# Second attention of a two-layer decoder trunk: filler remainders flushed together in mid head, one filler step ahead of transposes, Newton steps of two scalings moved

## Chip, cores and metric

One Trainium2 chip, one core. The metric is the time of one execution of the whole program in device microseconds, lower is better.

## What is computed

The reference is a decoder trunk of two layers over one sequence of 512 tokens with width 1024, in float32. Each layer has a token mixer and then a gated MLP with a causal convolution of width 3; each sub-layer starts with an RMS norm that is shifted and scaled by a vector c, and ends in a gated addition to x. The mixer of layer 0 is a stick-breaking attention. The mixer of layer 1, which the change is mostly about, is a sparse attention with an indexer:

```python
def dsa_attention(h, w_in, q_gain, k_gain, w_uv, w_out, rel_bias):
    proj = h @ w_in
    q, lat, qi, ki, wi = jnp.split(proj, [o1, o2, o3, o4], axis=-1)
    q = rms_norm(q.reshape(B, S, DSA_HEADS, DSA_LATENT), q_gain)
    k = rms_norm(lat, k_gain)
    ...
    logits = jnp.einsum('bqhd,bqkd->bqhk', qb, kg) * scale
    logits = logits + bias
    logits = jnp.where(valid[:, :, None, :], logits, NEG)
    p = jax.nn.softmax(logits, axis=-1)
    o_lat = jnp.einsum('bqhk,bqkd->bqhd', p, vg)
    ...
    o = jnp.einsum('bshl,hlv->bshv', o_lat, w_uv)
    return o.reshape(B, S, DSA_HEADS * DSA_V_DIM) @ w_out
```

There are 16 heads with a latent of 128. The query of each head is normalized over its 128 channels (`q_gain` goes into the keys), and the indexer picks 128 keys for each token.

## The kernel before

x stands transposed in SBUF, 8 tiles of 128 channels by 512 tokens. Every product with a weight is done as three matmuls (`mm3`, L247 to L250): weight and activation are each split into a high part and the remainder, and high by high, low by high and high by low are added up in PSUM. Weights come as chunks of 128x1024 by DMA; `split_hi` (L199) makes a chunk's high part on ScalarE, `split_lo` (L212) its low part, on VectorE or, where it is told so, on GpSimd. The order of the instructions of each engine is the order in which the code issues them; nothing reorders them later.

The program is a chain of `stick_layer`, `ffn_layer`, `dsa_layer`, `ffn_layer`. Between two of them stands `boundary` (L387, three times): the last product of a sub-layer in two halves of 256 tokens with 8 tiles each (`out_tile`, which adds to x by `add_to_x` on VectorE and squares on ScalarE), and beside it the next norm. The first half's norm is a seed on ScalarE (`norm_seed`, L324), one Newton step of three VectorE operations on 128x256 (`norm_newton`, L330) and 10 operations of a generator (`norm_ops`), of which a tuple says how many stand behind each tile of the second half. The mean squares of the second half are gathered in quarters by matmuls (`quarter_squares`, L300), which go on with the last four tiles' squares beside the next layer's first product.

The attention loop of `dsa_layer` (L1476) runs over 16 heads and is pipelined by a head. In the pass of head h, TensorE makes the logits of head n = h+1 in four row blocks j of 128 tokens by 128(j+1) keys (`logits`, three matmuls each; they use the two banks `z` in turn), and transposes head h's exponentials in three groups (`transposed`; the copy out of PSUM goes to ScalarE, VectorE, ScalarE). VectorE scales the logits by the query's factor, adds bias and mask and takes the row's maximum (`softmax`, L1372: L1376 and L1377); ScalarE makes the exponential and its row sum (`expo`, L1379). The factor is a column of `cols`, made by `q_norm` (L1129) from sums of squares: a seed on ScalarE and four VectorE operations on 128x16. GpSimd adds the mask to the biases of head h+2 behind each transposed group (`masked_bias`, L1350).

Two heads make a pair. In even heads from 2 on, `weighted` multiplies the previous pair's transposed exponentials by its values; `pair_values` stands in odd heads. The reciprocals of the row sums of a pair are spread out by a VectorE copy (`pair_sums`, L1429, tile `rvb`), transposed in `pair_scale` and multiplied in by `pair_hi`; `pair_lo` (VectorE, L1453, in odd heads from 3 on) makes the low part.

Where the loop calls `fill(n)`, n steps of the generator `late_steps` (L1317) are issued. A step is one `mm3`. The generator first makes the query projections of heads 12 to 15 (8 steps each, the first two of head 12 stand ahead of the loop), then the first half of the output projection (8 tiles of 4 steps). What has to follow each of these is put into the list `events`: behind a query `q_hi` (ScalarE: copy and square), `q_lo` (VectorE) with the next chunk's `split_hi`, and `split_lo` on GpSimd; behind the four queries `group_sum(3)`, `group_columns(3)` and `q_norm(12, 16)`; behind an output tile `add_to_x`. `fill` takes one event off the list after each step:

```python
def fill(n):
    for _ in range(n):
        next(filler, None)
        if events:
            events.pop(0)()
```

`LATE_STEPS` (L39) gives the number of steps of each head; half of them stand in mid head, ahead of the logits of block 2, the rest at its end.

Of the kernel before, what the change touches and what calls it, by code (L numbers as in the profile page):

```python
# [22 lines left out]
QT = S // P  # L23
# [4 lines left out]
HEADS = 16  # L28
# [9 lines left out]
EARLY_Q = 12  # L38
LATE_STEPS = [3, 3, 3, 3, 3, 2, 3, 3, 3, 4, 4, 4, 4, 4, 4, 4]  # L39
AHEAD = 2  # L40
# [77 lines left out]
def kernel_body(ctx, tc, xT, wst, cst, smalls, crow, ccol, relb, onehot, outT):  # L118
# [205 lines left out]
    def norm_seed(hf):  # L324
        ln = rstd[hf] = npool.tile([P, H2], F32, name="ln", bufs=2)
        act.activation(ln, sqs["pt"], AF.Abs_reciprocal_sqrt, bias=eps_c)
        rstd[hf, "ms"] = sqs["pt"]
# [59 lines left out]
    def boundary(last, O, l, gate, nxt, first):  # L387
# [51 lines left out]
        for m in range(KT):  # L439
            if m == 1:  # L440
                sum_squares(sqs["acc"], True, False)
                sum_squares(prev, False, True)
                norm_seed(0)
            if m == 5:
                quarter_squares(pend[:4], True)
            pend.append(out_tile(1, m))
            if m == 1:
                norm_newton(0)
            if m in (2, 4):
                split_hi()  # L450
            if m in (3, 5):
                split_lo()
            for _ in range((0, 0, 1, 1, 2, 1, 2, 2)[m]):
                next(ops0, None)
# [5 lines left out]
        hs, c = hcur["h"], halves[0]  # L460
# [599 lines left out]
    def dsa_layer(l, first, man):  # L1060
        with ExitStack() as st:
# [66 lines left out]

            def q_norm(h0, h1):  # L1129
                c = slice(h0 * QT, h1 * QT)  # L1130
                act.activation(rq[:, c], msq[:, c], AF.Abs_reciprocal_sqrt, bias=eps_c)
                dve.tensor_mul(r0q[:, c], rq[:, c], rq[:, c])
                dve.scalar_tensor_tensor(r0q[:, c], msq[:, c], EPS, r0q[:, c], op0=OP.add, op1=OP.mult)
                dve.scalar_tensor_tensor(rq[:, c], r0q[:, c], 3.0, rq[:, c], op0=OP.subtract, op1=OP.mult)
                dve.tensor_scalar(rq[:, c], rq[:, c], -0.5 * P ** -0.5, None, op0=OP.mult)

            ths = {}
# [6 lines left out]
            with ExitStack() as si:  # L1144
# [115 lines left out]
                steps = 2 * rounds  # L1260
# [47 lines left out]
            with ExitStack() as sa:  # L1308
# [8 lines left out]
                def late_steps():  # L1317

                    g, pt = late, late_pt
                    for h in range(EARLY_Q, HEADS):  # L1320
# [3 lines left out]
                        for _ in g:  # L1324
                            yield
                        events.extend([lambda h=h, pt=pt: q_hi(h, pt), lambda h=h, pt=pt: (q_lo(h, pt), split_hi()),
                                       lambda: split_lo(engine=pool)])
                    events.extend([lambda: group_sum(3), lambda: group_columns(3), lambda: q_norm(EARLY_Q, HEADS)])
                    for mp in range(4):
# [12 lines left out]
                def fill(n):  # L1342
                    for _ in range(n):
                        next(filler, None)
                        if events:
                            events.pop(0)()

# [112 lines left out]
                for j in range(QT):  # L1460
                    logits(0, j)
                    fill(1)
                    softmax(0, j)
                    if j == 0:
                        group_columns(2)
                        q_norm(8, EARLY_Q)
                        warm(AF.Exp)
                    expo(0, j)
                rvb = None

# [5 lines left out]
                for h in range(HEADS):  # L1476
# [9 lines left out]
                    if values:  # L1486
                        weighted(h - 2)
                    transposed(h, 0, True)
                    if more:
# [4 lines left out]
                    if not more:  # L1494
                        rvb = sums(h)
                        pair_values(h - 1)
                    fill(LATE_STEPS[h] // 2)
                    if more:
# [17 lines left out]
                    else:  # L1516
                        pair_scale(rvb)
                    fill(LATE_STEPS[h] - LATE_STEPS[h] // 2)
                    if values:
# [3 lines left out]
                pair_lo()  # L1523
                fill(100)
                first = boundary([("do", 1, m) for m in range(4)], O[4:], l, 2, (l, S_NF, 3, 4), up_first(l))
# [117 lines left out]
```

## Time and profile before

| | |
|---|---|
| Runs | 1291.43, 1288.93, 1291.10 us; median 1291.1 |
| The profiled execution | 1289.12 us |
| Its span | 1287.3 us, granted TensorE clock 1.00 |
| TensorE busy | 1267.7 us, 98% of the span, 6910 matmuls |
| VectorE busy | 930.0 us, 72% |
| ScalarE busy | 592.0 us, 46% |
| GpSimd busy | 103.4 us, 8% |
| DMA | 163.22 MB, 127 GB/s in the mean |

Times count from the start of the span. "Busy" is the time in which an engine executes an instruction; the weight loads of TensorE run beside its matmuls. The attention loop lies between about 760 and 895 us, the three boundaries near 260, 630 and 910 us.

### The profile page before, as it was taken

Reading aid. Unit: us, or ns where it says so; the run is one execution under the profiler, and the core shown is the slowest. Engines: PE = TensorE matmul, PEld = TensorE weight load, DVE = VectorE, ACT = ScalarE, POOL = GpSimd, SP = SyncE. Lnnn points to the kernel's source line nnn. Section 1 sums busy time; section 2 is a strip of 40 time slices with the busy share of each in tenths; the row PEclk is TensorE's granted clock in tenths of the full one; section 3 lists DMA queues with packets and bytes.
Section 4 is the critical chain, followed back from the end, with each engine's and each line's share of the span. In section 5 each row is a group of like instructions: output and inputs, shape, how many; then the busy total and the mean of one; then the engine's idle time right before and its main releaser. Section 6 shows DMA issues by size and latency. Waiting matters only on the chain.

```text
span 1287.3 us, 18011 instructions
## 1 busy us (share of the span) xinstructions
PE 1267.7 (98%) x6910; PEld 1054.8 (82%) x6910; DVE 930.0 (72%) x1528; ACT 592.0 (46%) x1051; POOL 103.4 (8%) x99
## 2 busy tenths in 40 slices
PE   8999999999999999999999999999999999999999
PEld 6988787898888888888897777767988888888888
DVE  5888988778777877885778897776876456456653
ACT  6576666454423323442555346654554334234430
POOL 0000000000000000000002355453000000000000
PEclk9999999999999999999999999999999999999999
DMA  9644434423575575654222212231322422423221
GB/s 374 212 131 132 140 124 126 136 66 117 194 250 188 181 239 191 195 177 151 83 66 82 82 50 58 66 120 52 92 86 74 127 86 74 128 89 98 75 90 66
DMA packets 50613, 163.22 MB, mean 127 GB/s; under 512 B 5808, under 2 KB 8624, under 8 KB 50528
## 3 DMA queue, kind: packets, MB, share of 16 engines
q1 hardware_dynamic: 50096, 161.30, 39.0%
q8 instruction: 54, 0.88, 0.3%
q10 hardware_dynamic: 432, 0.79, 0.2%
q14 instruction: 31, 0.25, 0.1%
HBM read 159.92 MB, written 2.14 MB: 126 GB/s over the span
## 4 chain that ended last, share of the span: by engine, by line
PE 89%; DVE 6%; ACT 2%; DMA 2%; issue 1%; SPq 0%; DVEq 0%; ACTq 0%
PE pt_u L248 11%; PE pt_u L249 11%; PE pt_u L250 11%; PE pt_d L248 5%; PE pt_d L249 5%; PE pt_d L250 5%; PE pt_first L248 2%; PE pt_first L249 2%; PE pt_first L250 2%; PE pt_q L248 2%; PE pt_qk L248 2%; PE pt_q L250 2%; PE pt_q L249 2%; PE pt_l L249 2%; PE pt_l L248 2%; PE pt_l L250 2%
## 5 line engine op out<-in xcount | busy, mean ns | idle before, releaser
L208 ACT ACTIVATE whi<-raw 128x1024 fp32r<-128x1024 f32 (+1 forms) x206 | 205.3, 1002 | 116.7 <-PE pt_d L250 93.2
L248 PE MATMUL pt_u<-hhi,whi 128*128 128x512 f32 x640 | 249.2, 389 | 0.0
L249 PE MATMUL pt_u<-hhi,wlo 128*128 128x512 f32 x640 | 249.0, 389 | 0.0
L250 PE MATMUL pt_u<-hlo,whi 128*128 128x512 f32 x640 | 249.0, 389 | 0.0
L216 DVE TENSOR_TENSOR wlo<-raw,whi 128x1024 fp32r<-128x1024 f32 (+1 forms) x186 | 213.9, 1151 | 14.1 <-ACT whi L208 13.3
L996 ACT ACTIVATE y<-pt_u,sm 128x512 f32<-128x512 f32 x80 | 62.2, 777 | 188.3 <-PE pt_u L250 188.3
L248 PEld LDWEIGHTS pt_u<-hhi,whi 128*128 128x128 f32 x640 | 120.1, 188 | 25.9 <-issue 1.1
L250 PEld LDWEIGHTS pt_u<-hlo,whi 128*128 128x128 f32 x640 | 120.1, 188 | 25.2
L249 PEld LDWEIGHTS pt_u<-hhi,wlo 128*128 128x128 f32 x640 | 120.1, 188 | 24.6
L997 DVE SCALAR_TENSOR_TENSOR y<-pt_u,sm,y 128x511 f32<-128x511 f32 x80 | 59.9, 748 | 97.1 <-ACT y L996 96.9
L248 PE MATMUL pt_d<-acthi,whi 128*128 128x512 f32 x288 | 112.0, 389 | 0.0
L249 PE MATMUL pt_d<-acthi,wlo 128*128 128x512 f32 x288 | 112.0, 389 | 0.0
L250 PE MATMUL pt_d<-actlo,whi 128*128 128x512 f32 x288 | 112.0, 389 | 0.0
L257 DVE SCALAR_TENSOR_TENSOR raw<-raw,cond 128x1024 f32<-128x1024 f32 x88 | 106.6, 1217 | 4.4 <-DMA raw<-wst 4.4
L370 DVE SCALAR_TENSOR_TENSOR x<-pt_d,mod,x 128x512 f32<-128x512 f32 x48 | 36.0, 750 | 72.8 <-PE pt_d L250 72.8
L232 ACT ACTIVATE acthi<-y 128x512 fp32r<-128x512 f32 x44 | 27.8, 632 | 105.4 <-DVE y L1015 105.4
L248 PE MATMUL pt_first<-hhi,whi 128*128 128x256 f32 (+1 forms) x224 | 68.2, 305 | 0.0
L249 PE MATMUL pt_first<-hhi,wlo 128*128 128x256 f32 (+1 forms) x224 | 67.1, 300 | 0.7 <-DVE wlo L216 0.7
L250 PE MATMUL pt_first<-hlo,whi 128*128 128x256 f32 (+1 forms) x224 | 66.9, 299 | 0.0
L250 PEld LDWEIGHTS pt_d<-actlo,whi 128*128 128x128 f32 x288 | 54.1, 188 | 11.3
L248 PEld LDWEIGHTS pt_d<-acthi,whi 128*128 128x128 f32 x288 | 54.1, 188 | 11.2
L249 PEld LDWEIGHTS pt_d<-acthi,wlo 128*128 128x128 f32 x288 | 54.1, 188 | 11.1
(252 smaller groups left out, 2691.7 us busy)
## 6 DMA issues: line engine op xcount, KB each, us to landing
raw<-wst SPq DMA_DIRECT2D x250, 512.0 KB, 3.7
raw<-wst SPq DMA_DIRECT2D x48, 384.0 KB, 3.0
th<-rb SPq DMA_DIRECT2D x16, 256.0 KB, 3.4
ada<-wst SPq DMA_DIRECT2D x4, 512.0 KB, 6.3
outT<-x SPq DMA_DIRECT2D x16, 128.0 KB, 1.7
x<-xT SPq DMA_DIRECT2D x5, 256.0 KB, 5.0
x<-xT ACTq DMA_DIRECT2D x3, 256.0 KB, 3.9
cond<-crow SPq DMA_DIRECT2D x1, 512.0 KB, 10.7
```

What stands on the lines that cost most here:

```text
L208: act.activation(hi[:, :n], raw[:, :n], AF.Copy)
L216: engine.tensor_sub(lo[:, :n], raw[:, :n], hi[:, :n].bitcast(F32))
L232: act.activation(hi, src, AF.Copy)
L248: pe.matmul(out, lhsT=whi, rhs=ahi, start=start, stop=False)
L249: pe.matmul(out, lhsT=wlo, rhs=ahi, start=False, stop=False)
L250: pe.matmul(out, lhsT=whi, rhs=alo, start=False, stop=stop)
L257: dve.scalar_tensor_tensor(raw, raw, 1.0, cond, op0=OP.mult, op1=OP.mult, accum_out=dst)
L370: dve.scalar_tensor_tensor(x[f][:, c], pt, mod[l][:, g * KT + f:g * KT + f + 1], x[f][:, c], op0=OP.mult, op1=OP.add)
L996: act.activation(y, pt, AF.Identity, scale=cw[2], bias=sm[:, b + S_CB + c:b + S_CB + c + 1])
L997: dve.scalar_tensor_tensor(y[:, 1:], pt[:, :S - 1], cw[1], y[:, 1:], op0=OP.mult, op1=OP.add)
```

## The change

- `fill` no longer takes events. A new function `flush` runs the events up to the next separator (`None`) in the list. It is called once in each head, in mid head ahead of the first fill, and a second time at the end of heads 9 and 10. Separators stand around `group_sum(3)`, `group_columns(3)` and `q_norm(12, 16)`, so that each flush does one of them.
- In heads without `weighted` (0 and the odd ones) one filler step stands ahead of the first group of transposes; it is taken from the head's number of steps. `LATE_STEPS` changes in heads 0, 4 and 6; its sum stays 54.
- `q_norm` is cut into `q_seed` and `q_newton`; for heads 8 to 11 the four VectorE operations move from the first block of head 0's logits behind the last one.
- In `boundary` the Newton step of the first half moves from behind the second half's tile 1 to directly behind the seed, ahead of the residual add of tile 1, and the tuple of operations behind the tiles changes.

```diff
--- before.py
+++ after.py
@@ -36,7 +36,7 @@
 H2 = S // 2
 QRING = 12
 EARLY_Q = 12
-LATE_STEPS = [3, 3, 3, 3, 3, 2, 3, 3, 3, 4, 4, 4, 4, 4, 4, 4]
+LATE_STEPS = [4, 3, 3, 3, 2, 3, 2, 3, 3, 4, 4, 4, 4, 4, 4, 4]
 AHEAD = 2
 FETCH = 1
 
@@ -441,16 +441,15 @@
                 sum_squares(sqs["acc"], True, False)
                 sum_squares(prev, False, True)
                 norm_seed(0)
+                norm_newton(0)
             if m == 5:
                 quarter_squares(pend[:4], True)
             pend.append(out_tile(1, m))
-            if m == 1:
-                norm_newton(0)
             if m in (2, 4):
                 split_hi()
             if m in (3, 5):
                 split_lo()
-            for _ in range((0, 0, 1, 1, 2, 1, 2, 2)[m]):
+            for _ in range((0, 1, 1, 1, 2, 1, 2, 1)[m]):
                 next(ops0, None)
         for _ in ops0:
             pass
@@ -1126,13 +1125,20 @@
                 act.activation(msq[:, 16 * g:16 * g + 16].rearrange("p (i j) -> p i j", i=4),
                                pt.rearrange("p (j i r) -> p i j r", j=QT, i=4)[:, :, :, 0], AF.Copy)
 
-            def q_norm(h0, h1):
+            def q_seed(h0, h1):
                 c = slice(h0 * QT, h1 * QT)
                 act.activation(rq[:, c], msq[:, c], AF.Abs_reciprocal_sqrt, bias=eps_c)
+
+            def q_newton(h0, h1):
+                c = slice(h0 * QT, h1 * QT)
                 dve.tensor_mul(r0q[:, c], rq[:, c], rq[:, c])
                 dve.scalar_tensor_tensor(r0q[:, c], msq[:, c], EPS, r0q[:, c], op0=OP.add, op1=OP.mult)
                 dve.scalar_tensor_tensor(rq[:, c], r0q[:, c], 3.0, rq[:, c], op0=OP.subtract, op1=OP.mult)
                 dve.tensor_scalar(rq[:, c], rq[:, c], -0.5 * P ** -0.5, None, op0=OP.mult)
+
+            def q_norm(h0, h1):
+                q_seed(h0, h1)
+                q_newton(h0, h1)
 
             ths = {}
 
@@ -1325,7 +1331,8 @@
                             yield
                         events.extend([lambda h=h, pt=pt: q_hi(h, pt), lambda h=h, pt=pt: (q_lo(h, pt), split_hi()),
                                        lambda: split_lo(engine=pool)])
-                    events.extend([lambda: group_sum(3), lambda: group_columns(3), lambda: q_norm(EARLY_Q, HEADS)])
+                    events.extend([None, lambda: group_sum(3), None, lambda: group_columns(3), None,
+                                   lambda: q_norm(EARLY_Q, HEADS)])
                     for mp in range(4):
                         whi, wlo = chunk(("do", 0, mp), 0)
                         for mi in range(2):
@@ -1342,8 +1349,14 @@
                 def fill(n):
                     for _ in range(n):
                         next(filler, None)
-                        if events:
-                            events.pop(0)()
+
+                def flush():
+
+                    while events:
+                        event = events.pop(0)
+                        if event is None:
+                            return
+                        event()
 
                 Ls = {}
 
@@ -1463,9 +1476,10 @@
                     softmax(0, j)
                     if j == 0:
                         group_columns(2)
-                        q_norm(8, EARLY_Q)
+                        q_seed(8, EARLY_Q)
                         warm(AF.Exp)
                     expo(0, j)
+                q_newton(8, EARLY_Q)
                 rvb = None
 
                 def sums(h):
@@ -1485,6 +1499,8 @@
                         expo(n, 0)
                     if values:
                         weighted(h - 2)
+                    else:
+                        fill(1)
                     transposed(h, 0, True)
                     if more:
                         softmax(n, 1)
@@ -1494,7 +1510,9 @@
                     if not more:
                         rvb = sums(h)
                         pair_values(h - 1)
-                    fill(LATE_STEPS[h] // 2)
+                    flush()
+                    steps = LATE_STEPS[h] - (not values)
+                    fill(steps // 2)
                     if more:
                         logits(n, 2)
                         softmax(n, 2)
@@ -1515,13 +1533,21 @@
                             load_bias(n + 3)
                     else:
                         pair_scale(rvb)
-                    fill(LATE_STEPS[h] - LATE_STEPS[h] // 2)
+                    if h in (9, 10):
+                        flush()
+                    fill(steps - steps // 2)
                     if values:
                         pair_hi()
                 weighted(HEADS - 2)
                 pair_hi()
                 pair_lo()
-                fill(100)
+                while events:
+                    flush()
+                for _ in filler:
+                    while events:
+                        flush()
+                while events:
+                    flush()
                 first = boundary([("do", 1, m) for m in range(4)], O[4:], l, 2, (l, S_NF, 3, 4), up_first(l))
         return first, man
 
```

In the following pieces `L` is a row block of logits and exponentials, `z` a bank of logits, `tr` a bank of transposes, `pt_q` the accumulator of a query projection, `q2l` its square, `whi` and `wlo` a weight chunk's two parts. The line numbers of the change are those of its own file.

TensorE in head 1, from the logits of head 2's block 1 on. Before:

```order
L1367 MATMUL z<-kph,qh 128x256
L1368 MATMUL z<-kph,ql 128x256
L1369 MATMUL z<-kpl,qh 128x256
L1391 MATMUL tr<-cons,L_7183 128x128
L1391 MATMUL tr<-cons,L_7185 128x128
L1391 MATMUL tr<-cons,L_7187 128x128
L1391 MATMUL tr<-cons,L_7189 128x128
L248 MATMUL pt_q<-hhi,whi 128x512
L249 MATMUL pt_q<-hhi,wlo 128x512
L250 MATMUL pt_q<-hlo,whi 128x512
```

With the change:

```order
L1380 MATMUL z<-kph,qh 128x256
L1381 MATMUL z<-kph,ql 128x256
L1382 MATMUL z<-kpl,qh 128x256
L248 MATMUL pt_q<-hhi,whi 128x512
L249 MATMUL pt_q<-hhi,wlo 128x512
L250 MATMUL pt_q<-hlo,whi 128x512
L1404 MATMUL tr<-cons,L_7183 128x128
L1404 MATMUL tr<-cons,L_7185 128x128
L1404 MATMUL tr<-cons,L_7187 128x128
L1404 MATMUL tr<-cons,L_7189 128x128
```

A step of the query projection that stood behind the first group of transposes (and others behind it) now stands between the logits and these transposes.

ScalarE from the end of head 0 to the exponential of head 2's block 2, in head 1. Before:

```order
L1381 ACTIVATE L_7189,sum<-L_7189,nm 128x512
L1088 ACTIVATE qh<-pt_q 128x512
L1089 ACTIVATE q2l<-pt_q 128x512
L1381 ACTIVATE L_7268,sum<-L_7268,nm 128x128
L1396 ACTIVATE pT<-tr 128x512
L1381 ACTIVATE L_7289,sum<-L_7289,nm 128x256
L208 ACTIVATE whi<-raw 128x1024
L1381 ACTIVATE L_7300,sum<-L_7300,nm 128x384
```

With the change:

```order
L1394 ACTIVATE L_7189,sum<-L_7189,nm 128x512
L1394 ACTIVATE L_7271,sum<-L_7271,nm 128x128
L1409 ACTIVATE pT<-tr 128x512
L1394 ACTIVATE L_7292,sum<-L_7292,nm 128x256
L1087 ACTIVATE qh<-pt_q 128x512
L1088 ACTIVATE q2l<-pt_q 128x512
L208 ACTIVATE whi<-raw 128x1024
L1394 ACTIVATE L_7303,sum<-L_7303,nm 128x384
```

The copy and the square of head 12's query, which stood ahead of head 2's first exponential, stand behind its second one, directly ahead of the split of the next weights.

GpSimd in head 1: the mask additions for head 3, and the low part of that weight chunk. Before:

```order
L1354 TENSOR_TENSOR L_7342<-th,maskb 128x128
L1354 TENSOR_TENSOR L_7366<-th,maskb 128x256
L1354 TENSOR_TENSOR L_7388<-th,maskb 128x384
L1354 TENSOR_TENSOR L_7390<-th,maskb 128x512
L216 TENSOR_TENSOR wlo<-raw,whi 128x1024
L1354 TENSOR_TENSOR L_7434<-th,maskb 128x128
```

With the change:

```order
L1367 TENSOR_TENSOR L_7343<-th,maskb 128x128
L216 TENSOR_TENSOR wlo<-raw,whi 128x1024
L1367 TENSOR_TENSOR L_7374<-th,maskb 128x256
L1367 TENSOR_TENSOR L_7396<-th,maskb 128x384
L1367 TENSOR_TENSOR L_7398<-th,maskb 128x512
L1367 TENSOR_TENSOR L_7437<-th,maskb 128x128
```

The low part of the weights stands behind the first mask addition, where it stood behind the fourth.

## Rows read from the trace of the kernel before

Each row of a timeline has the start in us, the duration in us, engine, line, operation, out<-in, the number of equal instructions in a row, and in brackets the idle time before it with what ended it.

**Rows 1.** The chain that ended last: shares of the span by engine.

```profile
PE 89%; DVE 6%; ACT 2%; DMA 2%; issue 1%; SPq 0%; DVEq 0%; ACTq 0%
```

**Rows 2.** Windows, attention: length; busy PE, PEld, DVE, ACT, POOL; clock; DMA share; GB/s.

```profile
760.00:895.00 135.00, 125.81 (x770) 98.33 (x769) 98.89 (x202) 81.93 (x216) 67.28 (x70) 1.00 0.23 71
```

**Rows 3.** Waits of TensorE, whole span: waiter <- releaser: idle sum, number, longest.

```profile
PE z L1367 <- DVE L L1376: 6.4, 8, 1.5
PE pt_part L305 <- ACT sqt L285: 3.0, 3, 1.0
PE tr L1391 <- ACT L L1381: 2.5, 4, 0.8
```

**Rows 4.** Timeline of TensorE: logits of block 3 that wait.

```profile
763.24 0.50 PE L1367 MATMUL z<-kph,qh 128*128 128x512 f32 x1 [1.28 <-DVE L L1376]
...
815.68 0.40 PE L250 MATMUL pt_q<-hlo,whi 128*128 128x512 f32 x1
817.60 0.44 PE L1367 MATMUL z<-kph,qh 128*128 128x384 f32 x1 [1.52 <-DVE L L1376]
```

**Rows 5.** Timeline of VectorE: a Newton operation of the query scales, first and last set.

```profile
760.69 1.09 DVE L1133 SCALAR_TENSOR_TENSOR cols<-cols 128x16 f32<-128x16 f32 x1
...
848.03 0.18 DVE L1133 SCALAR_TENSOR_TENSOR cols<-cols 128x16 f32<-128x16 f32 x1
```

**Rows 6.** Timeline of TensorE, heads 2 and 3.

```profile
783.47 0.48 PE L1367 MATMUL z<-kph,qh 128*128 128x512 f32 x1
...
785.16 0.40 PE L248 MATMUL pt_q<-hhi,whi 128*128 128x512 f32 x1
...
785.85 0.22 PE L1367 MATMUL z<-kph,qh 128*128 128x128 f32 x1
...
786.54 0.88 PE L1391 MATMUL tr<-cons,L 128*128 128x128 f32 x4
...
788.83 0.48 PE L1367 MATMUL z<-kph,qh 128*128 128x512 f32 x1
...
790.50 0.38 PE L1391 MATMUL tr<-cons,L 128*128 128x128 f32 x2
```

**Rows 7.** Timeline of ScalarE: last exponentials of a head; a query's square; a split.

```profile
786.22 0.72 ACT L1381 ACTIVATE L<-L,nm 128x512 f32<-128x512 f32 x1 [0.57 <-DVE nm L1377]
...
831.79 0.72 ACT L1381 ACTIVATE L<-L,nm 128x512 f32<-128x512 f32 x1 [0.57 <-DVE nm L1377]
...
834.88 0.59 ACT L1089 ACTIVATE q2l<-pt_q 128x512 f32<-128x512 f32 x1
835.36 1.06 ACT L208 ACTIVATE whi<-raw 128x1024 fp32r<-128x1024 f32 x1
```

**Rows 8.** Timeline of VectorE: heads 3 and 9.

```profile
790.67 0.43 DVE L1431 COPY rvb<-rv 128x512 f32<-128x512 f32 x1
...
835.50 0.69 DVE L1095 TENSOR_TENSOR ql<-pt_q,qh 128x512 fp32r<-128x512 f32 x1 [1.12 <-ACT q2l L1089]
...
838.02 1.43 DVE L1431 COPY rvb<-rv 128x512 f32<-128x512 f32 x1
...
839.37 0.74 DVE L1376 SCALAR_TENSOR_TENSOR L<-z,cols,L 128x512 f32<-128x512 f32 x1
```

**Rows 9.** Timeline of GpSimd and VectorE: a split of weights and what fell into it.

```profile
817.04 2.39 POOL L216 TENSOR_TENSOR wlo<-raw,whi 128x1024 fp32r<-128x1024 f32 x1 [1.73 <-issue]
...
818.63 1.35 DVE L1453 TENSOR_TENSOR olo<-bs,ohi 128x512 fp32r<-128x512 f32 x1
```

**Rows 10.** Timeline of ScalarE: table load ahead of the last query scales' seed.

```profile
846.11 1.28 ACT L1131 ACT_TABLE_LOAD   x1
```

**Rows 11.** Timeline of ScalarE and VectorE, third boundary: norm seed, residual adds.

```profile
908.93 0.46 ACT L326 ACTIVATE ln<-pt_norm,ecols 128x256 f32<-128x256 f32 x1
...
910.33 0.48 DVE L370 SCALAR_TENSOR_TENSOR x<-pt_l,mod,x 128x256 f32<-128x256 f32 x1 [1.82 <-PE pt_l L250]
...
921.76 0.48 DVE L370 SCALAR_TENSOR_TENSOR x<-pt_l,mod,x 128x256 f32<-128x256 f32 x1
```

## The prediction

> **What bounds the kernel now.** I read the chain that ended last first: TensorE holds 89% of it and no other engine more than 6% [rows 1]. So a microsecond counts only where TensorE stands still. Next, the windows: of the 135 us of the second attention TensorE is busy 125.8, at a granted clock of 1.00 [rows 2]. Then who waited for whom on TensorE [rows 3]: logits wait 8 times for VectorE's read of the block that last held their bank (6.4 us), transposes wait 4 times for ScalarE's exponential (2.5 us), and the quarter sums of the boundaries wait 3 times for a square (3.0 us). All twelve attention waits lie in the stretch that the change rearranges. A wait costs a little more than its idle time: from 815.68 to 817.60 is 1.92, where the usual pitch is 0.23, so 1.69 are lost for 1.52 shown [rows 4]. Twelve waits are thus 8.9 + 12 x 0.16 = 10.8 us. Five more odd heads end their first transposes about 0.2 late (786.54 to the next logits, 788.83, is one [rows 6]), 1.1 in all. **11.9 us** is what the change can win in the attention, less what waits remain or are new.
>
> **What it wins.** Query scales: at 760.69 a step of the Newton chain takes 1.09 where the same shape later takes 0.18 [rows 5], the logits of block 3 wait 1.28 behind it [rows 4]. With the four steps behind the last block's softmax that wait goes, and so do the two smaller ones that follow from it; the chain then stands beside a filler step. Step ahead of transposes: one step of three products is 0.69 (785.16 to 785.85 [rows 6]), no wait of the transposes is over 0.8 [rows 3]; so these four and the five small ones go, nearly. I leave 0.4 for all of them. The number of filler steps is the same, so TensorE's own work is.
>
> **What takes their place: odd heads.** After heads 1, 3, 7 and 9 a query projection is finished, and its copy, square, low part and the split of the next weights now stand together in mid head, ahead of the softmax of block 2. I follow head 9 of before, which already has that order. ScalarE: from the exponential of the last block (831.79) to the end of the square (834.88 + 0.59) is 3.7 [rows 7]. I take 3.9, since the copy of the transposes that precedes it comes behind one more filler step. VectorE can't start the low part earlier (835.50, right at the square's end), and block 2's and 3's softmax stand behind it: 2.52 from there to the copy `rvb` (838.02), 0.35 for that undisturbed (790.67 takes 0.43), 0.75 for the read of block 3 [rows 8]. So block 3's bank is free 3.9 + 2.5 + 0.35 + 0.8 = 7.6 after that exponential.
>
> On top comes GpSimd. Its split of weights takes 2.39, and a VectorE operation with both inputs in SBUF that fell into it (818.63) took 1.35, ending just after it [rows 9]; `rvb` at 838.02 took 1.43 for 0.43 in the same way, behind one of GpSimd's mask additions [rows 8]. The new order puts that split ahead of the masks, right behind ScalarE's split, which ends 0.95 after the square (835.36 + 1.06 [rows 7]). It then runs from 0.95 to 3.35 after the square, and `rvb` wants to start 2.55 after it: 0.8 more. Freed after **8.4**.
>
> TensorE's way to the product that needs this bank, from the logits of block 3 in the even head before [rows 6]: they, two transposes and a step 1.69; a second step 0.69; two logits 0.69; the inserted step 0.70; first transposes to the next block 3 2.29 less the 0.2 wait; that block and the values 1.67; transposes and one step (1.69 less 0.77) 0.92; a logit 0.28: 8.7. The exponential starts 2.75 after the same logits (783.47, 786.22 [rows 6, 7]), so TensorE arrives 6.0 after it. Before, such an odd head ended with two steps; the inserted one was taken from there. Wait: 8.4 - 6.0 = **2.4 in heads 1 and 3**. Head 7 follows a head with one step less: **3.1**. Head 9 keeps two steps and the sums ahead, as now, so I take a wait not far above the longest logits wait of now, 1.52 [rows 4]: **1.8**.
>
> **Heads 10 and 11.** The last query scales move from mid head to its end. There ScalarE needs a table load of 1.28 [rows 10] right behind the last exponential: 0.8 (as 831.79 [rows 7]) + 1.28 + 0.3 for a small seed, then on VectorE the Newton chain 0.8 (four steps as 848.03 [rows 5]), a residual add and the pair's scaling 1.3 (two operations of the low part's shape, 0.69 each) and block 0's read 0.35 (half of block 3's 0.74 [rows 8]), that is 4.85 after an exponential that started 2.75 behind its logits: 7.6. TensorE arrives with block 2 at about 4.9 (1.69 + 0.69 + 0.69 + 0.70 + transposes 0.4 + a step 0.75): **2.7**. The other table load delays that head's splits, and block 3's bank comes 1.0 late, or 2.0 if `rvb` falls into GpSimd's split (the two start within 0.3 of each other): **1.5**. Rows show no block longer than 1.0, and I go by that. The Trainium skill's page SBUF — State Buffer, section Who interferes with whom, says that the pair of ports is held for the whole instruction and the other engine fully blocks. By that rule head 11 could lose 3.0 in place of 1.5, and the total would be 1.5 higher.
>
> Head 13 gets a split and two residual adds in mid head: **0.6**. At the end of the loop nothing moves that TensorE waits for.
>
> **Boundaries.** VectorE idles 1.82 before 910.33 while the seed is there from 908.93 + 0.46 on [rows 11]; the three Newton steps, 1.25, move into it. But the first seven counts of the table now sum to 8, not 7, so one more pair of operations (0.8) stands ahead of the last residual add (921.76), whose square the quarter sums wait for, and 0.5 of the freed time goes into waiting for residuals that TensorE hasn't finished. Net about +0.1 each, +0.3 for three. Bounds: -0.5 (no waiting) to +0.8 (the move yields nothing) each.
>
> **Sum.** Left and new in the attention: 0.4 + 2.4 + 2.4 + 3.1 + 1.8 + 2.7 + 1.5 + 0.6 = 14.9. Against 11.9, and with +0.3: **+3.3 us**. The profiled execution took 1289.1, so 1292.4; the median of the runs, 1291.1, is 2.0 above it, so **1294.4**. Ends of the unknown: without any block by GpSimd the odd heads give 1.6 + 1.6 + 2.3 + 1.0, heads 11 and 13 1.0 and 0.1, together 10.7 and a net of -0.9; with head 11 at 2.0 and the boundaries at their worst +5.9.
>
> **Rivals.** First, *odd heads keep up* (faster). If the query's square ended 1.5 after the exponential, not 3.9, nothing would wait in heads 1, 3 and 7. Head 1 of before carries the same copies without a wait, which speaks for it; against it, they stand there ahead of the next head's first exponential and of the transposes' copy, now behind both. The 7.9 us would go: 1294.4 - 7.9 = 1286.5. It takes over from the point at which the low part starts before block 2's logits are done. Chance 0.20. Second, *an even trade*: the blocks don't happen, as with the `rvb` copy of 790.67 [rows 8], and the net is -0.9: 1290.2. Chance 0.30. Third, *the clock*: TensorE drops to the lower of its levels after a wait of 2.5 to 3 us. Now it is 1.00 across all waits up to 1.5 [rows 2, 3]. If it halved for the 8 us of one even head, that head would take 8 more: 1302. Chance 0.04. The Trainium skill's page TensorE: Matmul & The Clock Gate, section HAM oscillation, describes such drops after idle gaps; no run here shows one. The forecast, waits moved into odd heads, has 0.46; its own range is 1292 to 1297.5.
>
> **How the numbers follow.** About 0.2% of 1291.1, 2.6 us, is what a measurement of this kernel can tell from no change. Slower by more, above 1293.7: 0.36 of the forecast's 0.46 and the clock's 0.04, 0.40. Within: 0.10 of the forecast and 0.27 of the even trade, 0.37. Faster, below 1288.5: the first rival and 0.03 of the second, 0.23. The range leaves out half of the first rival and the far ends above: 1287 to 1297.5.
>
> **What would show it.** Right: TensorE's waits of logits on VectorE grow from 6.4 us, the longest at the second logits of heads 2, 4, 8 and at block 2 of head 11, while transposes wait almost nowhere and the start of the attention is some 2.7 us shorter; `rvb` copies of over 1 us beside GpSimd's splits in odd heads; quarter sums still near 3.0. Wrong: logits waits below 4 us, or a low part of the query that starts ahead of block 2's logits; then the first rival holds. If waits at heads 2, 4 and 8 are 1.5 each and no `rvb` is long, the second.

## The result

The changed kernel takes 1298.53 us (median of four runs, 1296.89 to 1299.11), the kernel before 1290.46 beside it (1288.93 to 1291.43): ratio 1.0062, 95% interval 1.0044 to 1.0079. It is slower, as forecast, but by 8.1 us where +3.3 was forecast, and outside the range that ended at 1297.5. The two profiled executions are 9.9 apart (1299.02 and 1289.12 us). Up to the first logits of the attention 1.0 of this has arisen (they start at 758.93, before at 757.93): 0.8 by 41 us of the program, in waits for parts of the first weight chunks, where the change touches nothing, and the rest in the first two boundaries. In the other profiles here the same matmul near 41 us comes between 0.1 earlier and 1.9 later than in the kernel before, so that part is chance.

The chain that ended last, of the changed kernel:

```profile
PE 89%; DVE 6%; ACT 2%; issue 1%; DMA 1%; SPq 0%; DVEq 0%; ACTq 0%
```

TensorE's share is what it was [rows 1]. The same 135 us as in [rows 2], and then stretches of 1 to 2 us of TensorE alone (length; PE busy; clock; DMA share; GB/s):

```profile
760.00:895.00 135.00, 122.06 (x719) 95.32 (x718) 94.82 (x195) 77.22 (x209) 65.45 (x70) 0.95 0.22 67
...
776.00:778.00 2.00, 0.82 (x6) 1.00 0.00 0
778.00:779.00 1.00, 0.09 (x1) 0.87 0.00 0
779.00:780.00 1.00, 1.00 (x5) 0.50 0.00 0
780.00:781.00 1.00, 1.00 (x4) 0.50 0.00 0
781.00:782.00 1.00, 1.00 (x4) 0.50 0.24 74
782.00:783.00 1.00, 1.00 (x12) 0.92 0.54 154
...
794.00:796.00 2.00, 0.61 (x5) 1.00 0.00 0
796.00:797.00 1.00, 0.28 (x2) 1.00 0.00 0
797.00:798.00 1.00, 1.00 (x7) 1.00 0.00 0
```

The granted clock is 0.95 where it was 1.00. It falls to 0.50, the lower of its two levels (1.2 for 2.4 GHz), behind the wait of head 2 (776.8 to 778.9) and stays there for some 3.4 us; behind the equally long wait of head 4 (794.6 to 796.7) it doesn't. Head 8 and head 11 show it again (head 11 here; length; busy PE, PEld, DVE, ACT, POOL; clock; DMA share; GB/s):

```profile
856.00:858.00 2.00, 0.00 (x0) 0.00 (x0) 0.68 (x5) 1.17 (x2) 0.00 (x0) 0.81 0.79 140
858.00:859.00 1.00, 0.27 (x1) 0.28 (x2) 1.00 (x3) 0.00 (x0) 0.00 (x0) 0.50 0.98 395
...
863.00:864.00 1.00, 1.00 (x7) 0.90 (x5) 0.42 (x1) 0.66 (x1) 0.21 (x1) 0.50 0.00 0
864.00:866.00 2.00, 2.00 (x16) 1.87 (x15) 1.93 (x5) 0.82 (x3) 2.00 (x1) 0.98 0.00 0
```

TensorE's waits, the lines that answer to [rows 3] (idle sum, number, longest; L1389 of the change is L1376 of before):

```profile
PE z L1380 <- DVE L L1389: 8.1, 6, 2.5
PE pt_o L248 <- DVE x L370: 3.5, 1, 3.5
PE pt_part L305 <- ACT sqt L285: 3.2, 3, 1.1
...
PE pt_o L248 <- DVE bs L1459: 1.3, 2, 0.8
```

The transposes' waits are gone; the logits wait six times instead of eight, but longer; a wait of 3.5 for a residual add and two for a pair's scaling are new.

I count lost time as the forecast did: from one matmul's start to the next, less the usual pitch. The waits of the attention are 12.4 us before and 14.4 after, so +2.0. What TensorE loses in slow matmuls rises by 1.6 in head 2, 1.55 in head 8 and 2.5 in head 11, so +5.6. A slow matmul is one that starts later than the usual pitch with no idle time before it. From the first logits to the first product of the boundary behind the attention it is 136.6 us before and 145.3 after, +8.7: these two make 7.6, the rest are pieces of under 0.6 that I don't assign. With the 0.8 of the program's start and 0.5 in the three boundaries that accounts for the 9.9.

### The profile page after: what moved, and what is told of

Same layout as the page of the kernel before. It is cut to its first block, busy times and chain, and to the rows that moved or that the text cites. A ratio compares the mean times of both kernels' runs of the same rounds, so it can differ in the third digit from the quotient of the medians.

```text
span 1297.2 us, 18005 instructions
## 1 busy us (share of the span) xinstructions
PE 1272.0 (98%) x6910; PEld 1057.1 (81%) x6910; DVE 930.3 (72%) x1528; ACT 591.4 (46%) x1051; POOL 105.3 (8%) x99
## 4 chain that ended last, share of the span: by engine, by line
PE 89%; DVE 6%; ACT 2%; issue 1%; DMA 1%; SPq 0%; DVEq 0%; ACTq 0%
PE pt_u L248 11%; PE pt_u L249 11%; PE pt_u L250 11%; PE pt_d L249 5%; PE pt_d L248 5%; PE pt_d L250 5%; PE pt_first L248 2%; PE pt_first L249 2%; PE pt_first L250 2%; PE pt_l L249 2%; PE pt_q L248 2%; PE pt_l L248 2%; PE pt_l L250 2%; PE pt_q L249 2%; PE pt_q L250 2%; PE pt_qk L248 2%
```

## Experiments

Each kernel was timed beside the kernel before on the same chip. A ratio is to that, the changed kernel's being 1.0062. "Head" is the pass of the loop, h.

**1. The boundaries alone.** The kernel before with this part of the change:

```diff
                 norm_seed(0)
+                norm_newton(0)
...
-            if m == 1:
-                norm_newton(0)
...
-            for _ in range((0, 0, 1, 1, 2, 1, 2, 2)[m]):
+            for _ in range((0, 1, 1, 1, 2, 1, 2, 1)[m]):
```

> The kernel before with the change of the boundaries alone. Theory (the 8 us are waits and a lower clock in the second attention): the quarter sums wait 3.0 to 3.3 us in all, the time is 0.3 us above before, within 0.2%. Rival (the boundaries cost more than the attention shows): 1.5 us or more above before, with quarter sums or first products that wait longer.

Measured: 1290.01 us, ratio 1.0001 (0.9993 to 1.0010). The quarter sums wait 3.2 us in all, against 3.0 [rows 3]. The boundaries are not where the time went.

**2. The query's square early.** The changed kernel, with copy and square of the queries 12 to 14 where they stood before the change:

```diff
-                        for _ in g:
+                        for k, _ in enumerate(g):
+                            if k == (5 if h == EARLY_Q else KT - 1):
+                                squares.append(lambda h=h, pt=pt: q_hi(h, pt))
                             yield
-                        events.extend([lambda h=h, pt=pt: q_hi(h, pt), ...
+                        events.extend([lambda: squares and squares.pop(0)(), ...
...
                     fill(steps - steps // 2)
+                    if h in (0, 2, 6):
+                        squares.pop(0)()
```

> The changed kernel, but the query's copy and square of heads 12 to 14 stand at the end of heads 0, 2 and 6, as before the change; low part and split of weights stay in mid head. Theory (ScalarE's late square is the larger part of the wait): the low part of head 1's query starts about 1.9 us sooner, the waits of 2.1, 2.1 and 2.5 at the second logits of heads 2, 4 and 8 shrink to 0.9 or less each, the clock stays at 1.00 there: some 8 us less than the changed kernel, about 1290.5. Rival (GpSimd's split is the larger part): waits of 1.5 or more stay, about 1295.

Measured: 1299.0 us, ratio 1.0068 (1.0054 to 1.0082): nothing won. The waits are 1.92, 2.08 and 2.43, hardly shorter. First the rows of head 1 in the changed kernel (ScalarE, VectorE, GpSimd, TensorE):

```profile
771.18 0.72 ACT L1394 ACTIVATE L<-L,nm 128x512 f32<-128x512 f32 x1 [1.06 <-DVE nm L1390]
...
773.87 0.59 ACT L1088 ACTIVATE q2l<-pt_q 128x512 f32<-128x512 f32 x1
774.35 1.06 ACT L208 ACTIVATE whi<-raw 128x1024 fp32r<-128x1024 f32 x1
...
774.50 0.69 DVE L1094 TENSOR_TENSOR ql<-pt_q,qh 128x512 fp32r<-128x512 f32 x1 [1.93 <-ACT q2l L1088]
...
777.02 1.17 DVE L1444 COPY rvb<-rv 128x512 f32<-128x512 f32 x1
778.12 0.74 DVE L1389 SCALAR_TENSOR_TENSOR L<-z,cols,L 128x512 f32<-128x512 f32 x1
...
775.55 2.37 POOL L216 TENSOR_TENSOR wlo<-raw,whi 128x1024 fp32r<-128x1024 f32 x1 [3.06 <-issue]
...
778.91 0.58 PE L1380 MATMUL z<-kph,qh 128*128 128x256 f32 x1 [2.09 <-DVE L L1389]
```

and then the same head in this experiment (VectorE, GpSimd, TensorE):

```profile
773.45 0.69 DVE L1094 TENSOR_TENSOR ql<-pt_q,qh 128x512 fp32r<-128x512 f32 x1 [0.42 <-ACT q2l L1088]
...
776.09 2.41 DVE L1447 COPY rvb<-rv 128x512 f32<-128x512 f32 x1
...
775.85 2.37 POOL L216 TENSOR_TENSOR wlo<-raw,whi 128x1024 fp32r<-128x1024 f32 x1 [2.93 <-issue]
...
779.21 0.39 PE L1383 MATMUL z<-kph,qh 128*128 128x256 f32 x1 [1.92 <-DVE L L1392]
```

Counted from the exponential of block 3 (771.63 here), the low part starts 1.82 behind it, not 3.32, and `rvb` 1.38 sooner than in the changed kernel. But that puts the copy 0.24 behind the start of GpSimd's split, and it takes 2.41 for 0.43: it ends 0.28 behind the split, as in the changed kernel (0.27). What was won ahead of the copy was waited away in it. The read of block 3 and TensorE follow as before.

**3. GpSimd's low part later.** The changed kernel with one separator more behind the first three queries:

```diff
-                                       lambda: split_lo(engine=pool)])
+                                       *[None] * (h < HEADS - 1), lambda: split_lo(engine=pool)])
```

> The changed kernel, but GpSimd's low part of the weights behind the queries 12 to 14 stands in the mid of the next, even head, where no spread copy follows. Theory (the spread copy rvb can't end before GpSimd's split does, and it is also late since the square is): with the split gone rvb takes 0.43 again and the waits at the second logits of heads 2, 4 and 8 fall from 2.1, 2.1 and 2.5 to about 1.3, 1.3 and 1.7, short enough that the clock stays at 1.00 there: 5 us less than the changed kernel, 1293.5. Rival (ScalarE's chain alone sets the end): waits within 0.2 of the changed kernel's.

Measured: 1298.17 us, ratio 1.0066 (1.0054 to 1.0079): a miss. VectorE and GpSimd of head 1:

```profile
776.58 1.13 DVE L1444 COPY rvb<-rv 128x512 f32<-128x512 f32 x1
...
775.37 2.05 POOL L1367 TENSOR_TENSOR L<-th,maskb 128x384 f32<-128x384 f32 x2 [1.28 <-PE tr L1404]
...
776.25 1.17 POOL L1367 TENSOR_TENSOR L<-th,maskb 128x512 f32<-128x512 f32 x1
```

With the split gone, the mask additions that had stood behind it move up into its place, and the copy is held by the second of them (the last row, which is part of the one above it): 1.13. The waits are 2.05, 2.05 and 2.04. The clock fell behind the second and the third of these, not behind the first.

**4. Both 2 and 3.** The edits are those two.

> Both at once: copy and square at the end of heads 0, 2 and 6, and GpSimd's low part one head later. Each alone leaves the other's delay; theory (two chains end at nearly the same time, so that only both together free the bank): waits of 0.4 or less at the second logits of heads 2, 4 and 8, no low clock there, some 9 us less than the changed kernel, 1289.5. Rival (the bank is late for a third reason): waits of over 1 stay.

Measured: 1290.97 us, ratio 1.0008 (0.9999 to 1.0017). Its waits of logits, all in all:

```profile
PE z L1383 <- DVE L L1392: 3.6, 6, 1.0
```

Head 2 has no wait over 0.3 left; heads 4 and 8 keep 0.93 and 0.96, where 0.4 was expected, and the clock stays up there. Of these two edits it takes both: either one alone leaves the copy inside GpSimd's work. In head 3 it still falls into a mask addition and takes 0.80.

**5. The spread copy later.** The changed kernel, with `rvb` behind the softmax of block 3 in odd heads:

```diff
-                        rvb = sums(h)
+                        sums(h)
                         logits(n, 3)
...
                         softmax(n, 3)
+                        if h % 2:
+                            rvb = pair_sums(heads[h][2])
                         expo(n, 3)
```

> The changed kernel, but the spread copy rvb stands behind the softmax of block 3 in odd heads, not ahead of it. Theory: the read of block 3 no longer stands behind the copy that GpSimd blocks, it starts right after the reciprocal, 1.1 sooner in head 1: waits of 2.1, 2.1 and 2.5 fall to about 1.0, 1.0 and 1.4, clock 1.00 there: 6 us less than the changed kernel, 1292.5. Rival (GpSimd's split also slows VectorE's softmax of block 3, which reads and writes SBUF too): the read itself takes over 1 us, and the waits stay at 1.5 or more.

Measured: 1290.31 us, ratio 1.0003 (0.9994 to 1.0012): the whole loss is back by moving one copy. VectorE and GpSimd of head 1, and the waits:

```profile
777.16 0.72 DVE L1389 SCALAR_TENSOR_TENSOR L<-z,cols,L 128x512 f32<-128x512 f32 x1
...
778.52 0.58 DVE L1444 COPY rvb<-rv 128x512 f32<-128x512 f32 x1
...
775.80 2.38 POOL L216 TENSOR_TENSOR wlo<-raw,whi 128x1024 fp32r<-128x1024 f32 x1 [3.08 <-issue]
```

```profile
PE z L1380 <- DVE L L1389: 3.4, 4, 1.2
```

The read of block 3 runs fully inside GpSimd's split and takes 0.72, where it takes 0.74 elsewhere; one of its inputs is in PSUM. In head 1 of the changed kernel, too, of VectorE's instructions that start inside the split the maximum (0.55), the copy out of PSUM (0.68) and the reciprocal (0.17) take what they took before, and only the copy from SBUF to SBUF is longer. The copy is still held a little here (0.58, by a mask addition), but nothing waits behind it for a bank. The waits are 0.84, 0.87 and 1.22 (expected 1.0, 1.0, 1.4), the clock stays up behind them, and the wait of 3.5 in head 11 is still there.

**6. The last query scales in mid head 10.** The changed kernel without one separator:

```diff
-                    events.extend([None, lambda: group_sum(3), None, lambda: group_columns(3), None,
+                    events.extend([None, lambda: group_sum(3), None, lambda: group_columns(3),
```

> The changed kernel, but the last query scales stand in mid head 10 right behind the columns, as before the change. Theory (table load, seed, Newton steps and the residual add behind them make the wait of 3.5 us in head 11): that wait is gone, with it the low clock behind it (2.1 us), and 0.6 to 1.3 us of new waits stand in head 10: about 4.5 us less than the changed kernel, 1294.0. Rival (the bank of the inserted step is late for another reason, the residual add in mid head): a wait of over 1.5 us at the inserted step of head 11 stays, and the time is within 1.5 us of the changed kernel's.

Measured: 1294.3 us, ratio 1.0034 (1.0022 to 1.0047), as expected. First the rows that make the 3.5 in the changed kernel (ScalarE, VectorE, TensorE), then the waits of the experiment:

```profile
855.58 1.28 ACT L1130 ACT_TABLE_LOAD   x1
856.88 0.31 ACT L1130 ACTIVATE cols<-cols,ecols 128x16 f32<-128x16 f32 x1
...
857.22 0.17 DVE L1134 TENSOR_TENSOR cols<-cols 128x16 f32<-128x16 f32 x1 [2.50 <-ACT cols L1130]
...
857.93 0.74 DVE L370 SCALAR_TENSOR_TENSOR x<-pt_o,mod,x 128x512 f32<-128x512 f32 x1
...
858.73 0.80 PE L248 MATMUL pt_o<-ohi,whi 128*128 128x512 f32 x1 [3.50 <-DVE x L370]
```

```profile
PE z L1380 <- DVE L L1389: 9.2, 8, 2.5
...
PE pt_o L248 <- DVE x L370: 0.8, 1, 0.8
```

Table load, seed, Newton chain, residual add: the inserted step of head 11 begins a new output tile, and its bank is the one that this residual add reads. In the experiment 0.8 of it is left, two more short waits of logits stand beside it, and the clock stays up in head 11. Here the clock fell in head 8 (wait of 2.45), and not in heads 2 and 4 (2.10 and 2.11). In head 2 it fell in the changed kernel, behind 2.09; this edit does nothing there, so some of the gain may be chance.

**7. TensorE kept busy.** The changed kernel with 8 products that nobody reads, where TensorE waits in heads 2, 4 and 8. They add work and leave everything else in place:

```diff
-                    av = pair["av"] = ptile([P, S], "av", "mm")
+                    if h + 2 not in (2, 4, 8):
+                        pair["av"] = ptile([P, S], "av", "mm")
+                    av = pair["av"]
...
                         for j in range(2):
                             logits(n, j)
+                            if h in (2, 4, 8) and j == 0:
+                                pair["av"] = ptile([P, S], "av", "mm")
+                                for _ in range(8):
+                                    pe.matmul(pair["av"], lhsT=kph[:, :P], rhs=kph, start=True, stop=True)
```

> The changed kernel with 8 useless products (1.8 us) between the first and the second logits of heads 2, 4 and 8, into a bank that the pair's values overwrite later: TensorE works where it stood still, and nothing ends sooner. Theory (the clock falls since TensorE stood still): clock 1.00 behind them in heads 2 and 8, waits left there 0.3 to 0.7, and 3.2 us less than the changed kernel although it does more, about 1295.3. Rival (the lower clock comes from something else at these places): the same time as the changed kernel, 1298.5, with the clock at 0.50 behind the wait as before.

Measured: 1296.52 us, ratio 1.0050 (1.0038 to 1.0063): 2.0 less than the changed kernel's median, for more work, where 3.2 was expected. The intervals of the two ratios overlap, so the time alone doesn't decide between theory and rival; the clock does. The same stretches behind the waits of heads 2 and 8:

```profile
778.00:780.00 2.00, 1.77 (x10) 1.00 0.00 0
780.00:782.00 2.00, 2.00 (x16) 1.00 0.03 8
...
824.00:826.00 2.00, 1.38 (x7) 1.00 0.00 0
826.00:828.00 2.00, 2.00 (x15) 1.00 0.00 0
```

The clock is 1.00 in both, and slow matmuls cost 2.63 and 2.63 in these heads, about what they cost before the change, where they cost 4.11 and 4.12: 3.0 in all. What is left of the waits is 0.2 to 0.6. In head 11, where nothing was filled in, the wait of 3.50 stays and the clock falls to 0.50 as before. The low clock comes from TensorE standing still, not from the place or from what other engines do there.

**8. The flush alone.** The kernel before with flush and separators, no inserted step, Newton steps and boundaries of before, and

```diff
-LATE_STEPS = [3, 3, 3, 3, 3, 2, 3, 3, 3, 4, 4, 4, 4, 4, 4, 4]
+LATE_STEPS = [4, 3, 4, 3, 2, 2, 2, 3, 4, 3, 4, 4, 4, 4, 4, 4]
```

> The kernel before with the flush alone: events in mid head, a second flush in heads 9 and 10, no inserted step, Newton steps and boundaries as before; the table of steps is set so that each query ends in the same head as in the changed kernel. Theory (the flush makes the new waits, and the old ones at the start and at the transposes stay): waits of 2.0 to 2.5 at the second logits of heads 2, 4 and 8, of 2.5 or more at block 2's logits of head 11, and the old 2.7 and 2.4 beside them: 1301, slower than the changed kernel. Rival (inserted step and flush make the waits together): waits below 1.5 in heads 2, 4 and 8, and a time within 3 us of before.

Measured: 1301.68 us, ratio 1.0082 (1.0067 to 1.0096). Its waits:

```profile
PE z L1381 <- DVE L L1390: 7.6, 7, 1.8
PE tr L1405 <- ACT L L1395: 3.5, 6, 0.8
...
PE pt_o L248 <- DVE x L370: 2.8, 1, 2.8
```

The time is as expected, the sizes are not: 1.42, 1.81 and 1.80 in heads 2, 4 and 8, and in their place more waits of transposes (3.5 us for 2.5) and two of 0.9 and 1.0 at the end of the loop that the expectation hadn't. So it came out by luck in part. The five executions lie between 1296.98 (granted clock 1.000) and 1302.29 (0.996); the profiled one took 1299.42. So without any low clock the flush's waits cost some 7 us, and the clock up to 5 more. The flush makes the waits in heads 2, 4 and 8, and the changed kernel with its inserted step (and another table of steps) has 0.3 to 0.7 more in each. That ScalarE's copy of the transposes, and the query's square behind it, come later by that step would explain it; it was not tried apart. The bank of the output tile is late here too (2.8, at the step in mid head 11, with the low clock behind it).

**9. The Newton steps alone.** The kernel before with `q_seed` at the first block and `q_newton(8, EARLY_Q)` behind the loop of head 0's blocks.

> The kernel before with the four Newton steps of heads 8 to 11 behind the last block's softmax, nothing else. Theory: the waits of 1.3, 0.3 and 0.6 us at the logits and transposes of the start (760 to 768 us) go and nothing else moves: 2.4 to 2.7 us less than before, 1287.3. Rival (the steps only wait elsewhere, ahead of head 1's softmax): within 1 us of before.

Measured: 1288.36 us, ratio 0.9988 (0.9979 to 0.9997). The logits' waits at the start go (6.4 in eight become 4.8 in six), the transposes' stay (2.6 against 2.5): 1.75 of lost time, not 2.7.

**10. Newton steps and inserted step, no flush.**

```diff
+                    else:
+                        fill(1)
                     transposed(h, 0, True)
...
+                    steps = LATE_STEPS[h] - (not values)
-                    fill(LATE_STEPS[h] // 2)
+                    fill(steps // 2)
```

> The kernel before with the two other parts of the attention's change: Newton steps behind the last block's softmax, and one filler step (with its event) ahead of the first transposes in heads without values; events still come one per step, the table of steps is the old one. Theory (these two parts win, the flush loses): the waits of 1.4, 0.5 and 0.8 at the start, and the transposes' of 0.7 to 0.9 go: 4 to 5 us faster than before, 1285.5. Rival (the inserted step's events delay the transposes' copy or the softmax): within 1.5 us of before.

Measured: 1289.3 us, ratio 0.9995 (0.9987 to 1.0004), a miss. Its waits of logits:

```profile
PE z L1374 <- DVE L L1383: 7.0, 9, 2.3
```

All transposes' waits are gone, but logits wait 0.9, 1.1 and 2.3 in heads 6, 7 and 8 (before: none, 1.5 and 1.3), and the clock fell behind the 2.3. There, too, a copy `rvb` took 1.37 beside mask additions.

**11. The same with the spread copy later.** Experiment 10 with the edit of 5.

> The kernel before with the Newton steps moved, one filler step and its event ahead of the first transposes, and the spread copy behind the softmax of block 3; no flush. Theory (what ate the gain of these parts were spread copies that GpSimd holds, 1.4 us in head 7): the waits of 0.8, 1.1, 1.3 and 2.3 at heads 2, 6, 7 and 8 shrink to 0.5 or less each: 4 to 5 us faster than before, 1285. Rival (something else is late at these places): within 1.5 us of before.

Measured: 1283.34 us, ratio 0.9950 (0.9936 to 0.9964): faster than both kernels. Its waits of logits:

```profile
PE z L1374 <- DVE L L1383: 3.5, 5, 1.1
```

Waits of 1.1 and 0.8 stay in heads 7 and 8; the others of that list are gone.

**12. Three orders together.** The changed kernel with the edits of 2, 5 and 6.

> The changed kernel with three orders of the runs so far: spread copy behind the softmax of block 3, copy and square at the end of heads 0, 2 and 6, last query scales in mid head 10. Theory (three separate causes add up): no wait over 0.5 in heads 2, 4 and 8, no wait of 3.5 in head 11, clock 1.00 throughout, waits of the attention some 5.5 us in all against 12.4 before: 6 to 7 us faster than before, 1283.5. Rival (the gains overlap, or new waits come up behind them): no faster than the best single one, 1290.

Measured: 1283.69 us, ratio 0.9953 (0.9940 to 0.9965), to be compared with 1283.5. Its waits:

```profile
PE z L1383 <- DVE L L1392: 1.5, 3, 0.6
PE pt_o L248 <- DVE bs L1462: 1.4, 2, 0.8
...
PE pt_o L248 <- DVE x L370: 0.8, 1, 0.8
```

4.8 us of lost time in the attention, where before it was 12.4, and the clock is 1.00 all through it. (In the profiled execution, 1284.97 us, the clock fell once, at 11 us of the program, behind a wait of 2.2 us for a square of x; the other four took 1283.19 to 1283.77.) The flush as such isn't slow: with the copy out of its way, the square early and the scales in mid head it reaches what experiment 11 reaches without it.

## Why the prediction was right or wrong

**Right: where TensorE would wait, and how long.** Lost time by the forecast's own terms:

| term | forecast | measured |
|---|---|---|
| start and transposes, what is left | 0.4 | none over 0.3 |
| second logits of heads 2, 4, 8 | 2.4, 2.4, 3.1 | 2.25, 2.27, 2.63 |
| behind head 9 | 1.8 | 0.61 + 0.67 |
| heads 10 and 11 | 2.7 + 1.5 | 3.66 |
| heads 13 to 15 | 0.6 | 0.67 + 0.62 + 0.99 |
| sum | 14.9 | 14.4 |
| of before | 11.9 | 12.4 |

That the sums come within 0.5 is luck in part: heads 2, 4 and 8 lose 0.75 less than forecast and heads 9 to 11 together 1.1 less, heads 13 to 15 1.7 more. The chain of head 1 ran as it was added up: low part to `rvb` 2.52, as forecast; bank free 7.7 after the exponential (771.18 to 778.91) against 8.4; TensorE there 5.6 after it against 6.0.

**Wrong: the clock, the third rival.** It had a chance of 0.04, a trigger "after a wait of 2.5 to 3 us" and a price of 8 for one head. The clock did fall, from waits of 2.09, 2.47 and 3.50, and the price was 1.6, 1.55 and 2.5: together 5.6 of the 9.9 between the profiled executions. The step that failed is the argument that the clock "is 1.00 across all waits up to 1.5": that held, but the forecast itself put waits of 2.4, 2.4, 3.1 and 2.7 in their place, all longer than any that the trace had shown, and went on with a clock at 1.00. Forecast (+3.3) and this term (+5.6) make 8.9. The Trainium skill's page TensorE: Matmul & The Clock Gate, section HAM oscillation, describes such drops behind idle gaps; the trace agrees with that, 1.00 before and 0.50 behind. Experiment 7 shows that standing still is the cause. What the trace of before said of the clock also held for one execution only (see the last section).

**Half right: head 11.** The moved scales do cost there, by the chain that was written down, table load, seed, Newton steps, residual add. But the forecast let block 2's logits be the first to wait. The first was the inserted step, since a new output tile needs the bank that the residual add reads. Part by part the forecast had looked at the step ahead as a gain only; of a step that is moved up, the bank that it writes is moved up too. The same shows in the small new waits of heads 13 and 15 (0.67 and 0.99), where it waits for the pair's scaling.

**Right in size, not in kind: GpSimd's hold on VectorE.** The forecast went by rows with no block over 1.0 and added 0.75 to 0.8 for each copy. In heads 1, 3 and 7 of the changed kernel that was so (1.17, 1.19 and 1.18 for 0.43). But it isn't a fixed surcharge: the copy ends just behind the GpSimd instruction into which it falls, so that 1.38 us won ahead of it in experiment 2 shortened TensorE's wait by 0.17. The Trainium skill's page SBUF — State Buffer, section Who interferes with whom, says that the other engine is fully blocked for the whole instruction; the row of 2.41 beside a split of 2.37 agrees.

**The first rival** (odd heads keep up) had the point at which it takes over wrong: an early square was not enough (experiment 2, no gain). **The second** (an even trade without the blocks) has nearly the time of experiment 5, 1290.31 for 1290.2, but not its sum: there the waits at heads 2, 4 and 8 are 0.84, 0.87 and 1.22 for the rival's 1.6, 1.6 and 2.3, and head 11 keeps its wait of 3.50 and the low clock. That the times agree is luck.

**Boundaries**: +0.3 forecast for three. In the traces of the changed kernel and of experiment 1 they take 0.5 longer (0.2, 0.1 and 0.2); in experiment 1's time that can't be told from nothing (+0.1 by the ratio, -0.9 to +1.3). **Newton steps**: the waits at the start went, but alone they were worth 1.75, not 2.7; with the inserted step the rest went too.

## What to carry to other kernels

A trace vouches for the clock only up to the longest wait that it holds, and only in the execution that it shows: where a plan makes a longer one, price the low clock behind it (here 1.5 to 2.5 us each) beside the wait. Before remainders are put together, look at which copies from SBUF to SBUF stand on VectorE between a bank and the engine that wants it, and put them behind the read of the bank: here one moved copy was worth 8 us. A step that fills a wait brings its own bank along, and needs that bank free at the earlier time.

## What was not expected of the hardware

Over all these profiles, behind waits of TensorE in the attention of up to 1.92 us the clock never fell; of eight waits of 2.04 to 2.11 it fell behind three; and behind all eleven of 2.29 or more. At equal length (2.05 three times over in experiment 3, to 0.01) it fell or not; what decides there stays open.

The kernel before isn't at 1.00 in every execution either. Of its 57 executions beside the experiments, the 11 that took 1290.73 us or more have a mean granted clock of 0.997 or 0.998, the 46 that took 1290.54 or less one of 0.999 or 1.000. So most of the 2 us by which the forecast set the median of the runs above the profiled execution seems to be the clock's, too; where it fell in those executions no trace shows.

GpSimd's hold ended at the same point each time: in head 1 the copy `rvb` ended 0.27 behind GpSimd's instruction in the changed kernel, 0.28 in experiment 2 and 0.29 in experiment 3, whether it had started 1.47, 0.24 or 0.33 behind that instruction's start. Over all fourteen profiles it is the same: the 70 copies `rvb` that took 0.53 us or more started inside a GpSimd instruction and ended 0.28 to 0.29 behind its end (the 0.27 above comes from rounded rows); the other 42 took 0.42 to 0.43, also where a GpSimd instruction started beside them. So a held copy's length tells how early it came, not how long it takes.
